# A list schedule with new prices: the same transformer trunk, its instructions in another order and partly on other engines

## The chip, the core and the metric

The kernel runs on one core of a Trainium2 chip. The metric is the device time of one execution in microseconds (us). A core has the matrix engine TensorE (PE in the profile; its weight loads are PEld), VectorE (DVE), ScalarE (ACT), GpSimd (POOL) and SyncE (SP), which here issues the DMA transfers. Each engine takes its own instructions strictly in the order in which they were issued, and waits at each for what it needs from the others.

## The reference, cut to what matters

Two layers over 512 tokens of width 1024, all in float32:

```python
for l in range(DEPTH):
    h = rms_norm(x, g_pre_mix[l])
    proj = h @ w_in[l]
    u_pool, q, k, v, iq, ik, iw = jnp.split(proj, SPLIT_POINTS, axis=-1)
    ...                                             # partial rotary embedding of q, k, iq, ik
    a_out = pool_mixer(u_pool, w_pool[l], pool_scale[l])
    b_out = dsa_attention(q, k, v, iq, ik, iw, topk)    # indexer scores, top 128 keys, softmax
    mix = jnp.concatenate([a_out, b_out], axis=-1) @ w_out[l]
    x = x + rms_norm(mix, g_post_mix[l])
    h = rms_norm(x, g_pre_ffn[l])
    f = jnp.square(jax.nn.relu(h @ w_ff1[l])) @ w_ff2[l]
    x = x + rms_norm(f, g_post_ffn[l])
```

## The kernel before

Every float32 product is made of three matmuls on operands split into a high part (a rounding copy) and a low part (a subtraction). The weights stream in: a DMA brings two chunks of 128 rows into a raw tile `wraw` (two such tiles), then for each chunk one copy and one subtraction write the two parts into a tile `ws`, of which there are eight. There are 200 chunks in a layer: 8 for the indexer (584 columns), 8 each for q, k, v and the pooling columns, 32 for `w_out`, 128 for the feed-forward part.

The text below calls the part of a layer from its first norm to the end of the `w_out` product and the next norm the **mix** (PE's products of the projections run beside DVE's indexer scores `sc`, the top-k selection `m`/`bias`, the rotary embedding `rt`, the splits `ihl`, `khl`, `qd` and the softmax `s`), and the rest the **feed-forward part**. The tiles `hT` and `A` belong to the norms before a product, `pn`, `rstd` and `x` to those after one, `facc` is the feed-forward sum, `fr` and `f1` its hidden values.

No engine's order is written by hand. The program is written down once, in program order; a recorder turns each call into an operation with a price in ns, an engine (or several that could take it) and the tiles that it reads and writes. The class `Planner` then runs a list schedule: 40 sweeps forward and backward in time, with prices from `cost`, hand-over times between engines from `LATENCY`, DMA times from `DMA_STARTS` and `DMA_LANDS`, and issues the instructions in the order of the best sweep. So the only thing that a table entry changes is the order on each engine's queue, and which of the possible engines takes an instruction. Three helpers leave that choice open: `tt` (an elementwise operation of two inputs in SBUF, DVE or POOL), `copy` (ACT or DVE) and `scaled` (DVE or ACT). Where there is a choice, `sooner` compares the time at which each engine would be done. The first way listed is the preferred one where time is short; another way is taken when the instruction would still be done `SPARE` ns before it is needed.

In the profile all these instructions have the line of the recorder (L349), so they are told apart by tiles.

Of the kernel before, what the change touches and what calls it, by code (L numbers as in the profile page):

```python
# [13 lines left out]
F32R = mybir.dt.float32r  # L14
# [67 lines left out]
class Planner:  # L82
    """Takes the instructions down in program order, finds what each depends on from the tiles that it
    reads and writes, and issues them in the order of a list schedule over the engines: of the
    instructions that an engine could start, the one with the longest chain of work behind it."""

    LATENCY = {("pe", "pe"): 0, ("pe", "act"): 197, ("pe", "dve"): 197,
               ("act", "act"): 34, ("act", "dve"): 152, ("act", "pe"): 377, ("act", "pool"): 170,
               ("dve", "dve"): 127, ("dve", "act"): 128, ("dve", "pe"): 362, ("dve", "pool"): 203,
               ("pool", "pool"): 102, ("pool", "dve"): 74, ("pool", "act"): 100, ("pool", "pe"): 309}  # L90
# [4 lines left out]
    SPARE = 4000.0  # L95
# [3 lines left out]
    NOISE = 500.0  # L99

# [40 lines left out]
    def either(self, *ways):  # L141
        """One instruction that several engines can take: each way makes one call."""
        self.collected = []
        for way in ways:
            way()
        found, self.collected = self.collected, None
        self.record([(e, c, f) for e, c, f, _, _ in found], found[0][3], found[0][4])
# [43 lines left out]
    def issue(self):  # L191
        """Sweeps forward and backward over the program in turn, each sweep taking its order of
        preference from the times of the one before, and issues in the order of the best. The first
        order is that of the longest chains behind, with a little noise to part equal ones."""
# [10 lines left out]
        for i in range(n - 1, -1, -1):  # L205
            e, cost, _ = ops[i][0][0]
            tail = 0.0
            for j, hard in succ[i]:
                tail = max(tail, rank[j] + (self.lag(e, ops[j][0][0][0]) if hard else -cost))
            rank[i] = cost + tail  # L210
# [15 lines left out]

    def sweep(self, key, pred, succ, late, fixed=None):
        """A list schedule. With ``fixed``, the ways are given and time runs backward."""
# [5 lines left out]
        for ways, _, _ in ops:  # L234
            for e, _, _ in ways:
                free[e], waiting[e], able[e] = 0.0, [], []

        def release(i):
            for w, (e, cost, _) in enumerate(ops[i][0]):
# [18 lines left out]
        def sooner(t, i, w):  # L258
            """Whether another engine should take instruction i."""
            mine = t + ops[i][0][w][1]  # L260
            for v, (e, cost, _) in enumerate(ops[i][0]):
# [18 lines left out]
        short = False  # L280
        while left:
# [34 lines left out]
            start[i], end[i], way[i] = t, t + ops[i][0][w][1], w  # L316
# [19 lines left out]
class _Recorder:  # L336
# [3 lines left out]
    def __getattr__(self, method):  # L340
        def call(*args, **kw):
            out = kw["out"] if "out" in kw else args[0]
            writes = [out] + ([kw["accum_out"]] if kw.get("accum_out") is not None else [])
            if method == "tensor_tensor_reduce":
# [4 lines left out]
                   lambda: getattr(self.real, method)(*args, **kw))  # L349
# [4 lines left out]
        return call  # L354

    def cost(self, method, args, kw, out, reads):
# [8 lines left out]
        if self.name == "pe":  # L365
            if method == "transpose":
                return 56 if args[1].dtype == F32R else 109
            return max(n / 2.4 + 2.5, 107 if free(args[1]) > 64 else 56)
# [8 lines left out]
        if self.name == "pool":  # L377
            if method == "memset":
                return 50
            return (70 + 1.2 * n) if method == "tensor_scalar" else (464 if n == 1 else 50 + 2.3 * n)  # L380
# [4 lines left out]
class WeightStream:  # L385
    """Chunks of weights in the order of their use: loaded, split into two float32r parts, and held
    in a ring until their last use."""
# [21 lines left out]
    def add_paired(self, src, r0, nrows, c0, ncols):  # L409
        """Chunks of 256 rows: rows r and r + 128 side by side."""  # L410
# [59 lines left out]
def hymba_trunk(ctx: ExitStack, tc: tile.TileContext, x, positions, g_pre_mix, w_in, w_pool,  # L470
# [60 lines left out]
    def tt(out, a, b, op, first="dve"):  # L531
        """an elementwise instruction on SBUF, on VectorE or GpSimd"""
# [3 lines left out]
    def copy(out, a):  # L536
        """a copy, on ScalarE or VectorE"""
        planner.either(lambda: act.activation(out, a, AF.Copy), lambda: dve.tensor_copy(out, a))

    def scaled(out, a, by):  # L540
        """rows times a scalar of each, on VectorE or ScalarE"""
# [109 lines left out]
    def square(out, a, total):  # L651
        """total = the sum of (a / 32) ** 2 along the row: a half's part of the row's mean square"""
        act.activation(out, a, AF.Square, scale=1.0 / 32.0, accum_out=total)

    def rstd_of(parts):
        """parts: [P, 2], the two halves' parts of the row's mean square"""
# [5 lines left out]
    def pre_norm(t, gain):  # L662
        """A[:, :, :, tile t] = the two parts of (RMSNorm(x[t]) * gain) transposed."""
# [22 lines left out]
    def post_norm(t, halves, gain, in_sbuf=False):  # L686
        """x[t] += RMSNorm(halves) * gain"""
# [21 lines left out]
    def rope(row, t, heads):  # L709
        """in place on the first 16 of each head's 64 columns."""  # L710
# [8 lines left out]
    def heads_stacked(dst_hl, row, heads):  # L719
        """dst[128, heads, 2, 64]: the two parts of each head side by side."""  # L720
# [4 lines left out]
    def heads_doubled(dst, row, heads):  # L725
        """dst[128, 2, heads, 2, 64]: either part of each head, twice side by side."""
# [4 lines left out]
    def transposed(dst, srcs):  # L731
        """dst [128, n, 128] <- transposes of n blocks of [128, 128] in float32r."""
# [14 lines left out]
    for l in range(DEPTH):  # L747
# [11 lines left out]
        # indexer projection, logits and scores  # L759
# [103 lines left out]
        # attention  # L863
# [118 lines left out]
        # feed-forward  # L982
# [102 lines left out]
```

## Time and profile before

| | before |
|---|---|
| runs | 1223.18, 1225.15, 1226.14 us; median 1225.15 |
| profiled execution | span 1222.7 us, 2.45 us under the median of the runs; no other time of that execution is given |
| PE, PEld busy | 1178.5 us (96%), 978.3 us (80%) |
| DVE busy | 777.1 us (64%) |
| ACT busy | 358.5 us (29%) |
| POOL busy | 668.5 us (55%) |
| instructions | 16265 |
| DMA | 115.41 MB, mean 94 GB/s |

A span runs from the first to the last instruction. An engine counts as busy while one of its instructions runs. A matmul's record is longer than the distance to the next one (in the feed-forward part 1393 of them start in 323 us, 0.232 us apart, while one record takes some 0.39 us), so a busy PE hides gaps shorter than about 0.16 us.

### The profile page before, as it was taken

To read this page: it belongs to the slowest core of one execution; us is meant where nothing else is said; L and a number is where in the kernel's file an instruction comes from. 1 tells how busy PE (TensorE), PEld (TensorE's weight loads), DVE (VectorE), ACT (ScalarE), POOL (GpSimd) and SP (SyncE) were. 2 spreads that over 40 slices of the span, in tenths; PEclk is the share of its full clock that TensorE was granted. 3 is DMA by queue.
4 is the path that set the end of the run, shared out by engine and by line. 5 is a ranking of instruction groups with operands and counts; after the bars stand their busy time and mean duration, and the time that the engine had idled before them with its cause. 6 is when DMAs were issued, how large, how long until landed. Compare 5 with 4: busy or idle time off the path is not lost.

```text
span 1222.7 us, 16265 instructions
## 1 busy us (share of the span) xinstructions
PE 1178.5 (96%) x5880; PEld 978.3 (80%) x5880; DVE 777.1 (64%) x1620; ACT 358.5 (29%) x840; POOL 668.5 (55%) x628
## 2 busy tenths in 40 slices
PE   5999999999999999999989999999999999999996
PEld 5987878788888888888887878787888888888885
DVE  8899999875216335245779999998632353343344
ACT  5444677540010000000354367675201000000011
POOL 4145331358659659558334543314785695684782
PEclk9999999999999999999999999999999999999999
DMA  7222222433332322332322222234234223323221
GB/s 242 70 56 67 69 69 88 138 105 121 106 101 69 121 86 71 119 93 90 113 70 69 69 69 69 71 104 138 86 104 121 87 83 107 104 86 104 87 87 69
DMA packets 62160, 115.41 MB, mean 94 GB/s; under 512 B 5248, under 2 KB 10368, under 8 KB 62080
## 3 DMA queue, kind: packets, MB, share of 16 engines
q1 hardware_dynamic: 62080, 114.38, 29.9%
q8 instruction: 46, 0.75, 0.3%
q14 instruction: 34, 0.28, 0.1%
HBM read 112.27 MB, written 2.10 MB: 94 GB/s over the span
## 4 chain that ended last, share of the span: by engine, by line
PE 68%; DVE 23%; issue 5%; POOL 1%; DMA 1%; ACT 0%; DVEq 0%; SPq 0%; POOLq 0%; ACTq 0%
PE pg L349 58%; DVE ws L349 4%; DVE bias L349 3%; PE pi L349 2%; DVE m L349 2%; PE pf L349 2%; DVE mx L349 2%; DVE sc L349 2%; DVE x L349 1%; DVE s L349 1%; DVE A L349 1%; DVE h L349 1%; DVE pT L349 1%; PE lg L349 1%; PE pool L349 1%
## 5 line engine op out<-in xcount | busy, mean ns | idle before, releaser
L349 POOL TENSOR_TENSOR ws<-wraw,ws 128x512 fp32r<-128x512 f32 x296 | 397.6, 1350 | 278.0 <-DVE ws L349 233.3
L349 DVE CAST ws<-wraw 128x512 fp32r<-128x512 f32 (+1 forms) x317 | 195.3, 624 | 337.1 <-PE pg L349 247.4
L349 PE MATMUL pg<-A,ws 128*128 128x512 f32 x1344 | 313.9, 395 | 0.0
L349 PEld LDWEIGHTS pg<-A,ws 128*128 128x128 f32 x1344 | 252.3, 188 | 60.0
L349 PE MATMUL pg<-ws,A 128*128 128x512 f32 x864 | 226.3, 400 | 1.9 <-DVE pn L349 1.6
L349 PE MATMUL pg<-ws,f 128*128 128x512 f32 x768 | 187.0, 394 | 0.0
L349 PEld LDWEIGHTS pg<-ws,A 128*128 128x128 f32 x864 | 156.9, 188 | 33.5 <-DVE pn L349 2.5
L349 PEld LDWEIGHTS pg<-ws,f 128*128 128x128 f32 x768 | 144.1, 188 | 33.6
L349 ACT ACTIVATE fr<-pg 128x512 f32<-128x512 f32 x49 | 27.9, 598 | 475.9 <-PE pg L349 475.1
L349 PE MATMUL pg<-ws,f1h 128*128 128x512 f32 x512 | 149.5, 394 | 0.0
L349 PEld LDWEIGHTS pg<-ws,f1h 128*128 128x128 f32 x512 | 96.1, 188 | 22.5
L349 POOL TENSOR_TENSOR rstd<-rstd,neg_half 128x1 f32<-128x1 f32 x32 | 25.9, 809 | 119.5 <-DVE rstd L349 114.9
L349 PE MATMUL pg<-ws,f1l 128*128 128x512 f32 x256 | 89.1, 393 | 0.0
L349 DVE TENSOR_TENSOR ws<-wraw,ws 128x512 fp32r<-128x512 f32 (+1 forms) x104 | 79.0, 772 | 0.9 <-ACT ws L349 0.5
L349 POOL TENSOR_TENSOR fr<-fr 128x512 f32<-128x512 f32 (+1 forms) x70 | 71.3, 1033 | 12.8 <-ACT fr L349 11.8
L349 ACT ACTIVATE s<-s,st 128x384 f32<-128x384 f32 (+3 forms) x96 | 54.0, 568 | 36.0 <-DVE st L349 32.5
L349 PE MATMUL pi<-ws,A 128*128 128x292 f32 x384 | 60.7, 305 | 2.2 <-DVE ws L349 1.8
L349 ACT ACTIVATE ws<-wraw 128x512 fp32r<-128x512 f32 (+1 forms) x83 | 51.9, 632 | 30.1 <-PE pg L349 19.8
L349 PE MATMUL pool<-A,ws 128*128 128x512 f32 x192 | 58.7, 407 | 0.0
L349 PEld LDWEIGHTS pg<-ws,f1l 128*128 128x128 f32 x256 | 48.1, 188 | 11.2
L349 PEld LDWEIGHTS pi<-ws,A 128*128 128x128 f32 x384 | 53.4, 190 | 3.7 <-DVE ws L349 2.4
L349 DVE CAST f1h<-fr 128x512 fp32r<-128x512 f32 (+1 forms) x40 | 39.2, 997 | 19.0 <-POOL fr L349 19.0
(154 smaller groups left out, 1493.7 us busy)
## 6 DMA issues: line engine op xcount, KB each, us to landing
wraw<-in_w_ff_dram SPq DMA_DIRECT2D x128, 512.0 KB, 3.7
wraw<-in_w_out_dram SPq DMA_DIRECT2D x32, 512.0 KB, 3.6
wraw<-in_w_in_dram SPq DMA_DIRECT2D x24, 512.0 KB, 3.6
wraw<-in_w_in_dram SPq DMA_DIRECT2D x8, 584.0 KB, 4.1
wraw<-in_w_in_dram SPq DMA_DIRECT2D x16, 256.0 KB, 3.0
x<-in_x_dram SPq DMA_DIRECT2D x4, 512.0 KB, 6.3
out_dram<-x SPq DMA_DIRECT2D x8, 256.0 KB, 2.0
gain<-in_g_pre_mix_dram SPq DMA_DIRECT2D x2, 512.0 KB, 4.7
```

The source lines that it names most:

```text
L349: lambda: getattr(self.real, method)(*args, **kw))
```

## The change

The program, its tiles and its arithmetic stay as they are. Changed are the planner's numbers and rules.

- Prices: a 512-column matmul costs 4.5 + 512/2.25 = 232 ns in the schedule in place of 215.8, small ones 60 or 111 in place of 56 or 107; a POOL elementwise operation 50 + 2.35 per column in place of 50 + 2.3, the one-column power 520 in place of 464.
- Hand-over times: to PE 240 ns from any engine in place of 309 to 377; PE to ACT and DVE 215 in place of 197; smaller moves between the others.
- `SPARE` is 20 us in place of 4 us.
- `copy` lists DVE first and ACT second; before it was the other way round.
- The forward sweeps know a port that DVE and POOL share. A method `port` gives each instruction a kind (0: does not use it; 1: uses it; 2: a DVE copy or row scaling with both sides in SBUF), and `shared` delays or lengthens it: kind 2 on DVE starts only when POOL is done and keeps POOL out until it ends; kind 1 on DVE becomes longer by 35% (`SLOWED`) of the time that it shares with POOL; a POOL instruction beside a DVE one becomes 10% longer.

```diff
-    LATENCY = {("pe", "pe"): 0, ("pe", "act"): 197, ("pe", "dve"): 197,
-               ("act", "act"): 34, ("act", "dve"): 152, ("act", "pe"): 377, ("act", "pool"): 170,
-               ("dve", "dve"): 127, ("dve", "act"): 128, ("dve", "pe"): 362, ("dve", "pool"): 203,
-               ("pool", "pool"): 102, ("pool", "dve"): 74, ("pool", "act"): 100, ("pool", "pe"): 309}
+    LATENCY = {("pe", "pe"): 0, ("pe", "act"): 215, ("pe", "dve"): 215,
+               ("act", "act"): 34, ("act", "dve"): 152, ("act", "pe"): 240, ("act", "pool"): 190,
+               ("dve", "dve"): 127, ("dve", "act"): 128, ("dve", "pe"): 240, ("dve", "pool"): 165,
+               ("pool", "pool"): 102, ("pool", "dve"): 100, ("pool", "act"): 150, ("pool", "pe"): 240}
...
-    SPARE = 4000.0
+    SPARE = 20000.0
...
+    SLOWED = 0.35
...
+    def shared(self, e, port, t, cost, held):
+        if e == "dve":
+            if port == 2:
+                t = max(t, held["pool"])
+                held["both"] = t + cost
+            else:
+                cost += self.SLOWED * min(cost, max(0.0, held["pool"] - t))
+            held["dve"] = t + cost
+        else:
+            t = max(t, held["both"])
+            if held["dve"] > t:
+                cost *= 1.1
+            held["pool"] = t + cost
+        return t, cost
...
-            start[i], end[i], way[i] = t, t + ops[i][0][w][1], w
+            cost, port = ops[i][0][w][1], ops[i][0][w][3]
+            if fixed is None and port:
+                t, cost = self.shared(e, port, t, cost, held_port)
+            start[i], end[i], way[i] = t, t + cost, w
...
+    def port(self, method, out, reads):
+        if self.name == "pool":
+            return 0 if method == "memset" else 1
+        if self.name != "dve" or any(a.space == bass.MemoryType.PSUM for a in [out] + reads):
+            return 0
+        if method in ("tensor_copy", "tensor_scalar"):
+            return 2
+        return 1 if method in ("tensor_tensor", "scalar_tensor_tensor") else 0
...
-            return max(n / 2.4 + 2.5, 107 if free(args[1]) > 64 else 56)
+            return max(4.5 + n / 2.25, 111 if free(args[1]) > 64 else 60)
...
-        planner.either(lambda: act.activation(out, a, AF.Copy), lambda: dve.tensor_copy(out, a))
+        planner.either(lambda: dve.tensor_copy(out, a), lambda: act.activation(out, a, AF.Copy))
```

Which engine splits the weight chunks, counted from the two orders (copy, then subtraction; "mix" is all chunks before the feed-forward ones):

| stage | copies before | copies now | subtractions before | subtractions now |
|---|---|---|---|---|
| layer 0 mix, 72 | DVE 35, ACT 37 | DVE 23, ACT 49 | DVE 43, POOL 29 | DVE 56, POOL 16 |
| layer 0 feed-forward, 128 | DVE 122, ACT 6 | DVE 25, ACT 103 | DVE 13, POOL 115 | DVE 39, POOL 89 |
| layer 1 mix, 72 | DVE 36, ACT 36 | DVE 26, ACT 46 | DVE 39, POOL 33 | DVE 54, POOL 18 |
| layer 1 feed-forward, 128 | DVE 124, ACT 4 | DVE 99, ACT 29 | DVE 9, POOL 119 | DVE 110, POOL 18 |

The first place is the program's start on SP's queue, where `x0` and `gain` feed the first norm, `wraw` is the first weights and `posi` the positions for the rotary tables. Before:

```order
L349 DMA x0_111<-in_x_dram 128x1024
L349 DMA posi_142<-in_positions_dram 128x4x1
L349 DMA gain_116<-in_g_pre_mix_dram 128x1024
L349 DMA wraw_117<-in_w_in_dram 128x2x584
L349 DMA x1_112<-in_x_dram 128x1024
L349 DMA wraw_118<-in_w_in_dram 128x2x584
```

Now:

```order
L371 DMA x0_111<-in_x_dram 128x1024
L371 DMA gain_116<-in_g_pre_mix_dram 128x1024
L371 DMA wraw_117<-in_w_in_dram 128x2x584
L371 DMA x1_112<-in_x_dram 128x1024
L371 DMA wraw_118<-in_w_in_dram 128x2x584
L371 DMA posi_142<-in_positions_dram 128x4x1
```

The positions went behind the second pair of weights, and the gain moved up one place. DVE at the same place, where `ropebuf` is the rotary tables' arithmetic, before:

```order
L349 TENSOR_TENSOR ropebuf_145<-posf_143,invt_144 128x32
L349 TENSOR_SCALAR ropebuf_145<-ropebuf_145 128x32 x2
L349 TENSOR_TENSOR ropebuf_145<-ropebuf_145 128x32
L349 SCALAR_TENSOR_TENSOR rstd_148<-ss_147 128x1
L349 TENSOR_SCALAR ropebuf_145<-ropebuf_145 128x32 x3
L349 TENSOR_TENSOR h_146<-x0_111,gain_116 128x512 x2
L349 TENSOR_TENSOR ropebuf_145<-ropebuf_145 128x32
L349 TENSOR_SCALAR h_146<-h_146,rstd_148 128x512
L349 CAST ws_119<-wraw_117 128x584
```

Now:

```order
L371 SCALAR_TENSOR_TENSOR rstd_148<-ss_147 128x1
L371 TENSOR_TENSOR h_146<-x0_111,gain_116 128x512 x2
L371 TENSOR_SCALAR h_146<-h_146,rstd_148 128x512
L371 CAST ws_119<-wraw_117 128x584
L371 TENSOR_TENSOR ws_119<-wraw_117,ws_119 128x584
L371 TENSOR_TENSOR ws_120<-wraw_117,ws_120 128x584
L371 TENSOR_TENSOR A_115<-hT_149,A_115 128x4x128
L371 TENSOR_TENSOR h_151<-x1_112,gain_116 128x512
```

The rotary arithmetic no longer stands among the first norm's instructions; the cast of the positions, which opens it, stands 14 rows further down.

The second place is DVE in layer 1's mix, from the scores of the second token tile (`sc1`) to the split `ihl_1095` of the third tile's indexer row, for which PE waits. Before:

```order
L349 CAST ws_1124<-wraw_996 128x512
L349 COPY irow_1092<-pi_1090 128x292
L349 SCALAR_TENSOR_TENSOR sc1_1073<-relu_1081,iw_1065,sc1_1073 128x256
L349 SCALAR_TENSOR_TENSOR sc1_1073<-relu_1083,iw_1065,sc1_1073 128x256
L349 TENSOR_TENSOR rt_1094<-irow_1092,cosT_140 128x144
L349 SCALAR_TENSOR_TENSOR sc1_1073<-relu_1085,iw_1065,sc1_1073 128x256
L349 CAST ws_1126<-wraw_1122 128x512
L349 TENSOR_TENSOR irow_1092<-rt_1094 128x9x8
L349 SCALAR_TENSOR_TENSOR sc1_1073<-relu_1087,iw_1065,sc1_1073 128x256
...
L349 CAST ws_1127<-wraw_1122 128x512
L349 TENSOR_TENSOR ihl_1095<-irow_1092,ihl_1095 128x8x64
```

Now:

```order
L371 COPY irow_1092<-pi_1091 128x284
L371 TENSOR_TENSOR ws_1127<-wraw_1122,ws_1127 128x512
L371 TENSOR_TENSOR rt_1094<-irow_1092,cosT_140 128x144
L371 SCALAR_TENSOR_TENSOR sc1_1073<-relu_1083,iw_1065,sc1_1073 128x256
L371 TENSOR_TENSOR rt_1094<-irow_1092,sinT_141 128x144
L371 SCALAR_TENSOR_TENSOR sc1_1073<-relu_1085,iw_1065,sc1_1073 128x256
L371 TENSOR_TENSOR ws_1130<-wraw_1125,ws_1130 128x512
L371 CAST ihl_1095<-irow_1092 128x8x64
L371 SCALAR_TENSOR_TENSOR sc1_1073<-relu_1087,iw_1065,sc1_1073 128x256
L371 TENSOR_TENSOR ihl_1095<-irow_1092,ihl_1095 128x8x64
```

The weight copies left DVE here (ACT has them), and weight subtractions that POOL made came to DVE; in layer 1's indexer stage POOL's queue now holds one weight subtraction (`ws_1129`) where it held five.

The third place is the end of DVE's queue: the last bank `pg_1844` is added to `facc`, multiplied by the gain (`pn_1854`), and the last token tile's `x3` is written. Before:

```order
L349 TENSOR_TENSOR facc_1601<-pg_1843,facc_1601 128x512
L349 TENSOR_TENSOR pn_1854<-facc_1601,gain_1549 128x512
L349 TENSOR_TENSOR pn_1851<-facc_1601,gain_1549 128x512
L349 SCALAR_TENSOR_TENSOR rstd_1853<-ss2_1852 128x1
L349 TENSOR_TENSOR facc_1601<-pg_1844,facc_1601 128x512
L349 SCALAR_TENSOR_TENSOR x2_113<-pn_1851,rstd_1853,x2_113 128x512 x2
L349 SCALAR_TENSOR_TENSOR rstd_1856<-ss2_1855 128x1
L349 SCALAR_TENSOR_TENSOR x3_114<-pn_1854,rstd_1856,x3_114 128x512 x2
```

Now:

```order
L371 TENSOR_TENSOR facc_1601<-pg_1843,facc_1601 128x512
L371 SCALAR_TENSOR_TENSOR x1_112<-pn_1848,rstd_1850,x1_112 128x512
L371 TENSOR_TENSOR pn_1851<-facc_1601,gain_1549 128x512
L371 SCALAR_TENSOR_TENSOR rstd_1853<-ss2_1852 128x1
L371 TENSOR_TENSOR facc_1601<-pg_1844,facc_1601 128x512
L371 TENSOR_TENSOR pn_1854<-facc_1601,gain_1549 128x512
L371 SCALAR_TENSOR_TENSOR x2_113<-pn_1851,rstd_1853,x2_113 128x512
L371 SCALAR_TENSOR_TENSOR rstd_1856<-ss2_1855 128x1
L371 SCALAR_TENSOR_TENSOR x2_113<-pn_1851,rstd_1853,x2_113 128x512
L371 SCALAR_TENSOR_TENSOR x3_114<-pn_1854,rstd_1856,x3_114 128x512 x2
```

One half of `pn_1854` stands right behind the last addition on DVE (POOL has the other half, ahead of it), and the last `rstd` stands between the two halves of `x2`.

## Rows read from the trace of the kernel before

**Rows 1.** Windows by stage: length, busy us (instructions) of PE, PEld, DVE, ACT, POOL, clock, DMA.

```profile
0.00:25.00 25.00, 12.21 (x71) 10.36 (x72) 19.82 (x47) 13.44 (x29) 11.00 (x40) 1.00 0.79 251
25.00:277.00 252.00, 244.14 (x1433) 208.38 (x1433) 231.71 (x582) 142.98 (x347) 90.88 (x109) 1.00 0.27 85
50.00:215.00 165.00, 159.98 (x863) 131.60 (x861) 162.52 (x437) 97.82 (x232) 60.10 (x75) 1.00 0.23 72
277.00:600.00 323.00, 323.00 (x1393) 261.21 (x1392) 135.74 (x187) 22.43 (x43) 221.31 (x174) 1.00 0.32 99
600.00:880.00 280.00, 265.63 (x1552) 228.68 (x1551) 255.97 (x615) 156.40 (x374) 112.49 (x122) 0.99 0.27 82
...
880.00:1200.00 320.00, 320.00 (x1382) 259.04 (x1381) 120.82 (x173) 19.04 (x35) 226.71 (x179) 1.00 0.31 96
```

**Rows 2.** Waits of the whole span: who waited for whom, us, times, longest.

```profile
DVE ws L349 <- DMA wraw<-in_w_ff_dram: 72.1, 24, 6.1
...
PE hT L349 <- DVE h L349: 13.0, 4, 9.4
...
PE hT L349 <- DVE rstd L349: 2.6, 1, 2.6
PE pi L349 <- DVE ws L349: 1.8, 3, 0.7
```

**Rows 3.** Timeline of the start: start, length, instruction, idle before it and releaser.

```profile
1.65 0.50 SPq L349 DMA_DIRECT2D gain<-in_g_pre_mix_dram  x1
...
7.46 1.29 DVE L349 TENSOR_TENSOR h<-x,gain 128x512 f32<-128x512 f32 x2 [1.22 <-DMA gain<-in_g_pre_mix_dram]
...
18.47 0.63 PE L349 MATMUL hT<-identf,h 128*128 128x128 f32 x4 [1.08 <-DVE ropebuf L349]
```

**Rows 4.** Timeline of layer 1's indexer stage.

```profile
648.20 0.47 DVE L349 SCALAR_TENSOR_TENSOR sc<-relu,iw,sc 128x256 f32<-128x256 f32 x1
...
649.09 1.30 POOL L349 TENSOR_TENSOR ws<-wraw,ws 128x512 fp32r<-128x512 f32 x1 [1.88 <-DVE ws L349]
649.30 2.29 DVE L349 SCALAR_TENSOR_TENSOR sc<-relu,iw,sc 128x256 f32<-128x256 f32 x2
...
653.14 1.48 DVE L349 SCALAR_TENSOR_TENSOR sc<-relu,iw,sc 128x256 f32<-128x256 f32 x1
...
656.04 0.54 PE L349 MATMUL tr<-ident,ihl 128*128 128x128 f32 x4 [3.03 <-DVE ihl L349]
```

**Rows 5.** DVE by form, 0 to 277 us: count, busy us, mean ns.

```profile
L349 DVE TENSOR_TENSOR ws<-wraw,ws 128x512 fp32r<-128x512 f32 x44 | 32.2, 747 | 0.2
L349 DVE CAST ws<-wraw 128x512 fp32r<-128x512 f32 x37 | 18.1, 494 | 2.7 <-DMA wraw<-in_w_out_dram 2.4
...
L349 DVE CAST qd<-qrow 128x512 fp32r<-128x512 f32 x7 | 2.9, 408 | 0.0
```

**Rows 6.** DVE by form, 600 to 880 us.

```profile
L349 DVE TENSOR_TENSOR ws<-wraw,ws 128x512 fp32r<-128x512 f32 x41 | 30.4, 751 | 0.2
L349 DVE CAST ws<-wraw 128x512 fp32r<-128x512 f32 x40 | 23.5, 592 | 5.4 <-PE pi L349 2.3 <-PE pg L349 1.9 <-DMA wraw<-in_w_out_dram 1.1
L349 DVE SCALAR_TENSOR_TENSOR x<-pn,rstd,x 128x512 f32<-128x512 f32 x14 | 13.0, 960 | 0.4 <-POOL rstd L349 0.4
...
L349 DVE SCALAR_TENSOR_TENSOR sc<-relu,iw,sc 128x256 f32<-128x256 f32 x7 | 5.6, 796 | 0.2
```

**Rows 7.** Instructions that write `ws`, 600 to 880 us: ns min/median/max, DVE, then POOL.

```profile
L349 DVE TENSOR_TENSOR ws<-wraw,ws x48: 667/683/1764, 602.5 to 876.0; 128x512 fp32r<-128x512 f32 x41, 128x584 fp32r<-128x584 f32 x7
...
L349 POOL TENSOR_TENSOR ws<-wraw,ws x35: 1276/1299/2056, 614.1 to 879.0; 128x512 fp32r<-128x512 f32 x34, 128x584 fp32r<-128x584 f32 x1
```

**Rows 8.** Timeline of the end.

```profile
1207.78 5.74 PE L349 MATMUL pg<-ws,f 128*128 128x512 f32 x24
...
1215.30 2.42 DVE L349 SCALAR_TENSOR_TENSOR x<-pn,rstd,x 128x512 f32<-128x512 f32 x2
1215.40 1.76 POOL L349 TENSOR_TENSOR pn<-facc,gain 128x512 f32<-128x512 f32 x1
...
1218.44 1.41 DVE L349 SCALAR_TENSOR_TENSOR x<-pn,rstd,x 128x512 f32<-128x512 f32 x2 [0.66 <-POOL rstd L349]
```

More of the change, by code (lines that the diff above doesn't have):

```diff
@@ L146, in either @@
         found, self.collected = self.collected, None
-        self.record([(e, c, f) for e, c, f, _, _ in found], found[0][3], found[0][4])
+        self.record([way[:4] for way in found], found[0][4], found[0][5])
     def record(self, ways, writes, reads):
@@ L205, in issue @@
         for i in range(n - 1, -1, -1):
-            e, cost, _ = ops[i][0][0]
+            e, cost = ops[i][0][0][:2]
             tail = 0.0
@@ L234, in sweep @@
         for ways, _, _ in ops:
-            for e, _, _ in ways:
+            for e, *_ in ways:
                 free[e], waiting[e], able[e] = 0.0, [], []
         def release(i):
-            for w, (e, cost, _) in enumerate(ops[i][0]):
+            for w, (e, cost, *_) in enumerate(ops[i][0]):
                 if fixed and fixed[i] != w:
@@ L260, in sooner @@
             mine = t + ops[i][0][w][1]
-            for v, (e, cost, _) in enumerate(ops[i][0]):
+            for v, (e, cost, *_) in enumerate(ops[i][0]):
                 if v == w:
@@ L280, in sweep @@
         short = False
+        held_port = {"pool": 0.0, "dve": 0.0, "both": 0.0}
         while left:
@@ L348, in call @@
             way = (self.name, self.cost(method, args, kw, out, reads),
-                   lambda: getattr(self.real, method)(*args, **kw))
+                   lambda: getattr(self.real, method)(*args, **kw), self.port(method, out, reads))
             if self.planner.collected is not None:
@@ L366, in cost @@
             if method == "transpose":
-                return 56 if args[1].dtype == F32R else 109
-            return max(n / 2.4 + 2.5, 107 if free(args[1]) > 64 else 56)
+                return 59 if args[1].dtype == F32R else 109
+            return max(4.5 + n / 2.25, 111 if free(args[1]) > 64 else 60)
         if self.name == "act":
@@ L379, in cost @@
                 return 50
-            return (70 + 1.2 * n) if method == "tensor_scalar" else (464 if n == 1 else 50 + 2.3 * n)
+            return (70 + 1.2 * n) if method == "tensor_scalar" else (520 if n == 1 else 50 + 2.35 * n)
         nbytes = math.prod(c for _, c in out.ap) * 4
```

## The prediction

> **What bounds the kernel now.** I read the windows by stage first, since the shares of the whole span mix stages with different limits. In the two feed-forward parts PE is busy for the whole stretch, 323.00 of 323 us and 320.00 of 320 [rows 1]: the other engines split weights beside it and none of their time is seen. That is over half of the span, and an order can't shorten it. In the mixes the reader is to see two full engines: between 50 and 215 us DVE is busy for 162.5 of 165 us while PE is busy for 160.0 [rows 1]. PE's idle time is 252.0 - 244.1 = 7.9 us from 25 to 277 us and 280.0 - 265.6 = 14.4 us from 600 to 880 us, together 22.3 us [rows 1]; ahead of them stand 12.8 us in the first 25 us [rows 1], of which 9.4 are the wait for the first norm [rows 2]; and after the last matmul, which ends at 1207.78 + 5.74 = 1213.5 us, 9.2 us remain to the end of the span [rows 8]. So what an order can win is 22 us in the mixes and a little at both ends.
>
> Then the list of waits: where PE waits it is for DVE [rows 2]. And the timeline shows why DVE is late: an instruction of 0.47 us takes 2.29 us for two, and 1.48 us for one, where a GpSimd subtraction of 1.30 us lies beside it [rows 4]. The same loss is in the means: weight copies on DVE take 494 and 592 ns against 408 for the same form that meets little [rows 5, 6], while DVE's median subtraction is 683 ns and its longest 1764 [rows 7].
>
> **The change part by part.** The sum is made against the profiled execution (span 1222.7 us) and its differences are then taken from the median of the runs, 1225.15.
>
> *The feed-forward parts: 0.* In layer 0 ACT takes 97 copies from DVE (6 to 103), in layer 1 DVE takes 101 subtractions from POOL (9 to 110). What hides them is PE's own work: layer 1's DVE, busy for 120.8 of 320 us [rows 1], gets 101 x 0.683 = 69 us more and is still at about 60%. If that cover fails, PE waits at a bank; this is a rival below.
>
> *The start: -2.5 us.* The gain's DMA was issued at 1.65 us, behind the 0.47 us of the positions' issue, and the first product of the norm waited for its landing at 7.46 us [rows 3]; it moves up by one issue. I take -0.5 for the first matmul, which comes at 9.4. Behind it PE waited 1.8 us in three pieces for split weights on DVE and 1.1 us behind the rotary arithmetic [rows 2, 3], which now stands lower in DVE's queue. Together 0.5 + 1.8 + 1.1 = 3.4 us at most; nothing at least, if the rotary tables are then late for the first indexer row. I take 2.5, since the tables' first user, the first token tile's `irow`, needs all eight weight chunks of the indexer first.
>
> *DVE's work in the mixes: -2.4 us.* From the table of the weight splits: POOL loses 13 + 15 = 28 subtractions, DVE gets them, at the present mean of 0.75 us [rows 5, 6] 28 x 0.75 = +21.0. DVE loses 12 + 10 = 22 copies, 22 x 0.408 = -9.0. Outside the weight and feed-forward tiles the order leaves DVE 11 instructions fewer (the most are five copies of `qd`), at the same 0.408 -4.5. That makes +7.5. Against it stands what DVE loses to POOL. Five groups show it, count times mean less the undisturbed time: 44 x (747 - 683) and 37 x (494 - 408) ns in layer 0; 41 x (751 - 683), 40 x (592 - 408), 7 x (796 - 470) and 14 x (960 - 705) ns in layer 1, the 705 being half of an undisturbed pair [rows 4 to 8]. That is 2.8 + 3.2 + 2.8 + 7.4 + 2.3 + 3.6 = 22.1 us. POOL's busy time in the mixes (11.0 + 90.9 + 112.5 = 214.4 us [rows 1]) falls by 28 x 1.30 = 36 us, 17%; its weight subtractions there fall from 62 to 34, by 45%. Lower bound of the relief: 17% of 22.1 = 3.8. Upper bound: all of it, if what remains on POOL is put where DVE does nothing that it disturbs. I take 45%, 9.9, because the long subtraction is what stands beside the stretched instructions. Net 7.5 - 9.9 = -2.4, between +3.7 and -14.6.
>
> *Two waits that hang on a stretched DVE instruction: -5.6 us.* At the second place of the order, PE waited 3.03 us for `ihl` [rows 4]. DVE lost 2.29 - 0.94 = 1.35 and 1.48 - 0.47 = 1.01 us ahead of it; now POOL has one weight subtraction in this stage in place of five, and DVE's own exchange there is small (a few subtractions against as many copies). The other is the 2.6 us before `hT` at the layer's start, behind an `rstd` [rows 2]. Both can stay (0) or other waits of the 22.3 us can go too; I take these two, 3.0 + 2.6.
>
> *The end: -1.0 us.* The last two additions to `x2` took 2.42 us beside a POOL product, and an undisturbed pair 1.41 [rows 8]. Now DVE makes the last half of that product itself, right behind the last addition, so 1.0 us goes; between 0 and 2 (the last `rstd` also comes forward).
>
> *The other prices* have no term of their own: they act only through the order.
>
> Sum: -2.5 - 2.4 - 5.6 - 1.0 = -11.5 us. From 1225.15 this is 1213.6 us, 0.9% less.
>
> A rule speaks against this. The Trainium skill, page "SBUF — State Buffer", section "SBUF: two separate sides", says that VectorE and GpSimd share a pair of ports as an exclusive lock: a DVE instruction with two inputs in SBUF, too, waits until a GpSimd instruction is done, and does not share. By that rule the planner's 35% is too little for a subtraction, and the sum would be that of the first rival. Of the rows, the longest subtraction agrees with the page: 1764 ns is an undisturbed one of 683 and most of a GpSimd one of 1299 [rows 7]. The mean of 751 [rows 6] says that few meet.
>
> **The rivals.**
> *Slower: the subtractions that came to DVE run into POOL.* Priced as lengthened by 35% of the overlap, they may be put beside the 34 weight subtractions and the other work that POOL keeps. If each of the 28 waits for half of a 1.30 us instruction, 0.65 in place of the 0.07 in the mean, DVE gets +16.3 us; with the -2.4 this is +14, and the two waits stay. 1225.15 - 2.5 - 1.0 + 14 = 1236. The lock of the Trainium skill's page "SBUF — State Buffer" would make it so wherever the two meet. It decides from 7 us of net growth on DVE. For it: DVE is full there, and the longest instruction shows that full waits occur [rows 1, 7]. Against it: POOL has less to meet, and in 85 of them the mean loss was under 0.07 us [rows 5, 6].
> *No measurable difference: what the mixes gain is lost in the feed-forward parts.* ACT, which emptied PE's banks at once, has the copies in the same queue, and copies wait for weights: DVE's did so 24 times, up to 6.1 us [rows 2]. If each of the 16 blocks of hidden values lost 0.6 us to a copy ahead of it, 10 us come back: 1225.15 - 11.5 + 10 = 1223.7. Against it: a bank and a weight tile are both freed by PE's progress, so the plan keeps their order even when it is late.
> *A larger gain.* If the schedule with truer prices leaves no PE idle time in the mixes, -22.3, with -3.4 and -2 at the ends: 1197.5. For it speaks that every price of PE was too low by some 7% (215.8 planned, 232 in the rows: 323 us for 1393 matmuls [rows 1]). Against it: PE and DVE are both nearly full, and an order must fit both.
>
> **How the numbers follow.** Likeliest 0.55, with its own range from 1205 (two thirds of the larger gain) to 1221; the larger gain 0.14, 1197 to 1205; no measurable difference 0.18; slower 0.13. About 0.3%, 3.7 us, is what a measurement of this kernel can tell from no change. Faster is 0.55 + 0.14 = 0.69. From 1200 to 1228 leaves out the slower case and half of the larger gain, 0.2.
>
> **What would show it.** The first `hT` at about 8.9 us instead of 9.4 and no wait behind `ropebuf` in the first 25 us; POOL's busy time in the mixes down to some 175 us; weight copies on DVE there nearer to 408 than to 592 ns; no wait of some 3 us before `tr`; both feed-forward parts still with PE full; about 8 us from the last matmul to the end. It would be wrong if DVE's mean subtraction in the mixes goes well above 0.75 us, if PE shows idle time between 277 and 600 us, or if PE's idle time in the mixes stays near 22 us although DVE got faster: then it was not DVE that held it.

## The result: 0.7% slower, where 0.9% faster was predicted

The changed kernel takes 1232.92 us (1232.19 to 1234.36) against 1224.22 us of the kernel before beside it: a ratio of 1.007, 95% interval 1.0056 to 1.0084. Its profiled execution, the slowest of the four runs (1234.36), has a span of 1232.6 us. The windows by stage, cut at 285 and 890 us in place of 277 and 880, since the work is later (columns as in [rows 1]):

```profile
0.00:25.00 25.00, 15.43 (x91) 14.10 (x92) 19.33 (x33) 14.47 (x31) 12.31 (x41) 1.00 0.80 262
25.00:285.00 260.00, 245.63 (x1414) 209.40 (x1413) 233.88 (x589) 156.52 (x372) 70.89 (x92) 0.99 0.26 81
285.00:600.00 315.00, 315.00 (x1357) 254.34 (x1356) 85.82 (x115) 88.43 (x148) 152.73 (x118) 1.00 0.31 98
600.00:890.00 290.00, 276.96 (x1588) 236.21 (x1587) 256.36 (x614) 171.76 (x410) 90.72 (x109) 0.99 0.27 84
890.00:1200.00 310.00, 310.00 (x1337) 250.82 (x1336) 167.07 (x253) 44.71 (x81) 56.82 (x43) 1.00 0.31 98
```

Both feed-forward parts are full as before. The start is better: PE idles for 9.6 us of the first 25, not 12.8. Layer 0's mix is worse, 260.0 - 245.6 = 14.4 us idle for 7.9, and layer 1's a little better, 13.0 for 14.4 [rows 1]. The list of waits says where (PE's waits, with total, times and longest as in [rows 2]):

```profile
PE hT L371 <- ACT h L371: 8.8, 3, 8.0
PE tr L371 <- ACT kS L371: 3.7, 1, 3.7
PE tr L371 <- DVE ihl L371: 2.6, 4, 1.3
...
PE tr L371 <- ACT khl L371: 2.5, 1, 2.5
...
PE tr L371 <- DVE khl L371: 1.7, 1, 1.7
```

The longest wait before `tr` behind `ihl`, 3.03 us [rows 4], is down to 1.3, and the first `hT` comes at 8.0 in place of 9.4. New are three waits in the evacuation of the k projection (1.65 and 3.70 us in layer 0, 2.5 us in layer 1). `evac_k` copies a bank to `krow`, applies the rotary embedding (`rt`), splits it (`khl`), transposes it on PE (`tr`) and copies the result to `kS`. The timeline of that place in layer 0:

```profile
109.65 2.74 POOL L371 TENSOR_TENSOR ws<-wraw,ws 128x512 fp32r<-128x512 f32 x2
...
111.17 1.76 DVE L371 TENSOR_TENSOR khl<-krow,khl 128x512 fp32r<-128x512 f32 x1
112.35 0.90 POOL L371 TENSOR_TENSOR rt<-krow,sinT 128x128 f32<-128x128 f32 x1
112.86 0.55 DVE L371 MAX8 m<-bias 128x8 f32<-128x384 f32 x1
...
113.08 0.50 PE L371 MATMUL tr<-ident,khl 128*128 128x128 f32 x4 [1.65 <-DVE khl L371]
113.21 2.56 POOL L371 TENSOR_TENSOR ws<-wraw,ws 128x512 fp32r<-128x512 f32 x2
113.33 1.31 DVE L371 TENSOR_TENSOR rt<-krow,cosT 128x128 f32<-128x128 f32 x1
...
114.02 1.17 PE L371 MATMUL pg<-ws,A 128*128 128x512 f32 x4
114.56 1.76 DVE L371 TENSOR_TENSOR khl<-krow,khl 128x512 fp32r<-128x512 f32 x1
...
117.21 0.63 ACT L371 ACTIVATE khl<-krow 128x512 fp32r<-128x512 f32 x1 [4.88 <-DVE krow L371]
...
118.26 1.06 ACT L371 ACTIVATE kS<-tr 128x512 fp32r<-128x512 f32 x2
...
118.89 0.75 PE L371 MATMUL tr<-ident,khl 128*128 128x128 f32 x4 [3.70 <-ACT kS L371]
...
120.46 1.92 PE L371 MATMUL pg<-ws,A 128*128 128x512 f32 x4
```

A split of 0.67 us takes 1.76 twice, since it runs only when POOL's weight subtraction is over; `rt` waits on POOL's queue behind two of them; and on ACT the copy `kS` stands behind a `khl` that waited 4.88 us for `krow`. PE has four matmuls of its own left, then waits. Behind the wait the same four matmuls take 1.92 us in place of 1.17: the granted clock fell to 0.50, which is 1.2 GHz. Three such stretches of the changed kernel, the second with the wait ahead of it (ahead of the first PE had waited for 0.67 us, ahead of the third for 2.45):

```profile
40.20:43.61 3.41, 3.36 (x14) 3.36 (x15) 2.14 (x9) 0.93 (x2) 0.49 (x2) 0.50 0.02 5
114.02:118.89 4.87, 1.17 (x6) 0.64 (x5) 4.87 (x12) 1.68 (x4) 1.75 (x2) 0.98 0.65 203
118.71:122.12 3.41, 3.23 (x13) 2.73 (x14) 3.41 (x10) 1.81 (x4) 0.00 (x0) 0.50 0.01 5
716.04:722.87 6.83, 6.41 (x26) 5.28 (x26) 6.32 (x12) 2.87 (x6) 3.69 (x4) 0.50 0.42 120
```

Of the kernel before there is one such stretch ahead of the end, behind a wait of 1.9 us:

```profile
787.48:790.89 3.41, 3.14 (x15) 3.17 (x16) 2.48 (x13) 1.02 (x3) 0.00 (x0) 0.50 0.43 148
```

So 13.65 us at 1.2 GHz in place of 3.41: at most (13.65 - 3.41) / 2 = 5.1 of the 9.9 us between the two spans. Idle time is another 2.0 (+5.1 in the mixes net, -3.2 at the start, +0.1 at the end); 2.8 us remain that no row places. These stretches differ from execution to execution: over the four runs the mean granted clock lies between 0.992 and 0.996.

### The profile page after: what moved, and what is told of

Same layout as the page of the kernel before. It is cut to its first block, busy times and chain, and to the rows that moved or that the text cites. A ratio compares the mean times of both kernels' runs of the same rounds, so it can differ in the third digit from the quotient of the medians.

```text
span 1232.6 us, 16141 instructions
## 1 busy us (share of the span) xinstructions
PE 1186.3 (96%) x5880; PEld 983.5 (80%) x5880; DVE 778.9 (63%) x1627; ACT 480.8 (39%) x1054; POOL 388.0 (31%) x407
## 4 chain that ended last, share of the span: by engine, by line
PE 73%; DVE 18%; issue 3%; ACT 2%; DMA 2%; POOL 1%; POOLq 0%; DVEq 0%; SPq 0%; ACTq 0%
PE pg L371 61%; DVE ws L371 4%; DVE bias L371 3%; PE pi L371 2%; DVE m L371 2%; PE pf L371 2%; PE pool L371 2%; DVE sc L371 2%; PE po L371 2%; PE tr L371 1%; PE s L371 1%; DVE x L371 1%; PE pt L371 1%; DVE s L371 1%; PE hT L371 1%
## 5 line engine op out<-in xcount | busy, mean ns | idle before, releaser
L371 POOL TENSOR_TENSOR ws<-wraw,ws 128x512 fp32r<-128x512 f32 (+1 forms) x141 | 193.6, 1375 | 380.4 <-DVE ws L371 195.4
L371 ACT ACTIVATE ws<-wraw 128x512 fp32r<-128x512 f32 (+1 forms) x227 | 141.4, 632 | 324.8 <-PE pg L371 253.5
L371 PE MATMUL pg<-ws,A 128*128 128x512 f32 x864 | 231.8, 404 | 2.2 <-DVE pn L371 1.3
L371 DVE TENSOR_TENSOR ws<-wraw,ws 128x512 fp32r<-128x512 f32 (+1 forms) x259 | 202.0, 791 | 16.9 <-ACT ws L371 12.9
L371 DVE CAST ws<-wraw 128x512 fp32r<-128x512 f32 (+1 forms) x173 | 82.5, 478 | 189.7 <-PE pg L371 160.7
L371 PE MATMUL pg<-ws,f 128*128 128x512 f32 x768 | 191.1, 394 | 0.0
L371 DVE TENSOR_TENSOR facc<-pg,facc 128x512 f32<-128x512 f32 x48 | 31.4, 687 | 79.7 <-PE pg L371 79.6
L371 ACT ACTIVATE s<-s,st 128x384 f32<-128x384 f32 (+3 forms) x102 | 57.9, 570 | 34.4 <-DVE st L371 33.5
L371 POOL TENSOR_TENSOR fr<-fr 128x512 f32<-128x512 f32 (+1 forms) x41 | 40.6, 1007 | 94.4 <-ACT fr L371 63.7
L371 POOL TENSOR_TENSOR rstd<-rstd,neg_half 128x1 f32<-128x1 f32 x32 | 21.6, 677 | 114.1 <-DVE rstd L371 113.9
```

The costliest lines, as they stand in the source:

```text
L371: lambda: getattr(self.real, method)(*args, **kw), self.port(method, out, reads))
```

## The experiments

All times are medians; each ratio is against the kernel before, run beside it, with a 95% interval. The theories are named in the expectations. **1**: VectorE's two-input instructions wait out GpSimd's. **2**: luck of one order. **3**: the new hand-over times. **4**, formed after the first four runs: the old, too low TensorE price was a slack.

**Four subtractions moved by hand.** `issue` gives four named operations to VectorE after the plan is made:

```diff
+        for i in (849, 863, 879, 893):
...
+            way[i] = [w[0] for w in ops[i][0]].index("dve")
         for i in sorted(range(n), key=lambda i: (start[i], i)):
```

> The changed kernel with four GpSimd weight subtractions of the k projection's evacuation in layer 0 (the ones at 109.7 and 113.2 us of its trace, two each) given to VectorE at the same places of the order; nothing else moves. Theory 1 (VectorE's two-input instructions wait out GpSimd's in full, and this is the place where it costs most): the two 1.76 us subtractions of khl go to 0.68, the waits of 1.65 and 3.70 us before tr shrink to under 2 together, the drop of the granted clock behind them goes, and the time falls by 4 to 8 us, to 1225 to 1229. Theory 2 (order luck: this scheduler's orders scatter by a per cent whatever the prices): the four subtractions add 2.7 us to a full VectorE, the stall moves on, and the time stays within 2 us of 1233. Theory 3 (hand-over to TensorE priced at 240 ns where it takes more): the waits before tr stay, since nothing of the hand-over is changed, within 2 us of 1233.

1230.01 us, ratio 1.0044 (1.0029 to 1.0059), outside all three ranges. The two `khl` splits took 0.68 us and the clock stayed at 1.00 there, as theory 1 says, but the waits fell from 1.65 and 3.70 to 1.5 and 2.2 us only. Theory 1 has the right instructions and a third of the loss, 2.9 us; the interval still overlaps that of the changed kernel (from 1.0056), so even this third is hardly clear of the noise. The clock isn't all the edit's doing: the stretch at 40.20 us, where the order is the same, is at 1.00 here too.

**The port rule as a full lock.**

```diff
-        return 1 if method in ("tensor_tensor", "scalar_tensor_tensor") else 0
+        return 2 if method in ("tensor_tensor", "scalar_tensor_tensor") else 0
```

> The changed kernel with one number of its port rule changed: two-input VectorE instructions on SBUF count as kind 2, so in the plan they wait until GpSimd is done and keep it out, in place of being lengthened by 35% of the overlap. Theory 1: the plan now fits the chip, no instruction of 0.68 us takes 1.76 on VectorE in the mixes, and the time falls below that of the kernel before, 1205 to 1220. Theory 2: some other order, 1217 to 1240 with no relation to the rule. Theory 3: the waits before tr stay as many and as long as now (about 15 us over the span), 1228 to 1236.

1241.43 us, ratio 1.0137 (1.0122 to 1.0152). All weight splits of layer 0's mix went to ACT and POOL. The windows of its first two stages:

```profile
0.00:25.00 25.00, 10.90 (x63) 9.77 (x64) 7.84 (x18) 16.84 (x34) 18.31 (x46) 1.00 0.78 254
25.00:285.00 260.00, 246.90 (x1376) 208.77 (x1375) 172.60 (x453) 168.02 (x392) 179.87 (x196) 0.97 0.27 82
```

VectorE is busy for 172.6 of 260 us, and PE still idles for 13.1, so VectorE's load doesn't set the time there. Its meetings with POOL did not go on the chip, though: in the same 260 us an addition to `x` takes 1268 ns on the mean, where an undisturbed pair took 1.41 us [rows 8]:

```profile
L371 DVE SCALAR_TENSOR_TENSOR x<-pn,rstd,x 128x512 f32<-128x512 f32 x8 | 9.8, 1268 | 0.3 <-POOL rstd L371 0.3
```

And PE idles for 14.1 us of the first 25, 4.5 more than in the changed kernel: over half of what the full lock costs is lost at the start, where POOL's queue now holds the first norm's product and two weight subtractions ahead of the power for its `rstd`. Theory 1's range is missed, but a run that keeps the meetings doesn't settle it.

**No port rule** (the condition `if fixed is None and port` made false).

> The changed kernel without the port rule (new prices, hand-over times, SPARE and the order of the copies stay). Theory 1: without any price for the port VectorE meets GpSimd more often, mean weight subtraction on VectorE in the mixes above that of the changed kernel, 1234 to 1245. Theory 2: within 8 us of 1233 on either side. Theory 3: as now, 1230 to 1236, since the hand-over prices are the cause and they stay.

1241.87 us, ratio 1.0139 (1.0122 to 1.0156): with the new prices the rule is worth 9 us. The time lies in theory 1's range, but its reason does not hold: VectorE's mean weight subtraction is 721 and 741 ns in the two mixes, below the changed kernel's 770 and 796 (shown further down). Theories 2 and 3 miss.

**Another seed** (`SEED = 54`).

> The changed kernel with another seed for the noise that parts equal chains in the first sweep (54 in place of 53). Theory 1 and theory 3: the same prices make the same kind of order, so slower than the kernel before again, 1228 to 1237. Theory 2: the time differs from 1233 by over 4 us and can fall on the other side of 1224.

1231.73 us, ratio 1.006 (1.0045 to 1.0075): 1.2 us from seed 53, with quite another order (VectorE has 1513 instructions in place of 1627). Theory 2 is weak.

**TensorE's old prices in the changed kernel.**

```diff
-                return 59 if args[1].dtype == F32R else 109
-            return max(4.5 + n / 2.25, 111 if free(args[1]) > 64 else 60)
+                return 56 if args[1].dtype == F32R else 109
+            return max(n / 2.4 + 2.5, 107 if free(args[1]) > 64 else 56)
```

> The changed kernel with TensorE's old prices (a 512-column matmul at 215.8 ns in place of 232), all else as changed. Theory 4, new (the old numbers were wrong by a slack: TensorE was planned too fast, so in the true run every other engine was ahead of it, and a late instruction seldom stopped it): the slack comes back, TensorE's idle time between 25 and 120 us falls from 8.2 us to under 4, and the time falls by 6 us or more, to 1218 to 1227. Theory 1 (waits behind GpSimd, wherever they fall): the number of meetings hardly changes, within 3 us of 1233. Theory 2 (order luck): within 3 us too, going by the 1.2 us that another seed made.

1215.92 us, ratio 0.9931 (0.9914 to 0.9949): 17.0 us from TensorE's prices, and faster than both kernels. PE's idle time between 25 and 120 us fell from 8.2 to 2.5 us. Theories 1 and 2 miss; theory 4 has the direction, with 2 us more than its range. Its windows of the mixes, and the same place of the timeline as above:

```profile
25.00:285.00 260.00, 251.60 (x1451) 213.68 (x1450) 232.78 (x573) 157.83 (x379) 89.34 (x111) 1.00 0.28 87
...
600.00:890.00 290.00, 282.64 (x1626) 241.26 (x1625) 259.93 (x602) 173.80 (x411) 116.00 (x127) 1.00 0.28 90
```

```profile
105.20 3.94 PE L371 MATMUL pg<-ws,A 128*128 128x512 f32 x16
105.22 1.78 DVE L371 TENSOR_TENSOR khl<-krow,khl 128x512 fp32r<-128x512 f32 x1
...
108.98 0.54 PE L371 MATMUL tr<-ident,khl 128*128 128x128 f32 x5
...
112.20 3.47 PE L371 MATMUL pg<-ws,A 128*128 128x512 f32 x14
...
112.93 1.47 DVE L371 TENSOR_TENSOR khl<-krow,khl 128x512 fp32r<-128x512 f32 x1
...
115.51 0.46 PE L371 MATMUL tr<-ident,khl 128*128 128x128 f32 x4
```

The same split is stretched nearly as much, 1.78 and 1.47 us. But it ends at 107.00 and 114.40, and PE comes to its transposes at 108.98 and 115.51, after 16 and 14 matmuls of its own: no wait, and no clock below 1.00 until PE's last matmul.

**The old hand-over times** (the table of before).

> The changed kernel with the old table of hand-over times (362 and 377 ns to TensorE in place of 240), all else as changed. Theory 3 (240 ns to TensorE takes away a slack that the old 362 to 377 gave): the waits before tr go, 1220 to 1227. Theory 4: the 122 to 137 ns are small against the 7% on each of TensorE's matmuls, so a part at most, 1227 to 1233. Theory 2: within 3 us of 1233.

1236.89 us, ratio 1.0104 (1.0086 to 1.0122): theory 3 falls. The new table is worth 4.0 us, which none of the expectations held.

**SPARE at 4 us.**

> The changed kernel with SPARE at 4 us in place of 20, all else as changed. The plan then leaves nearly all weight splits of the mixes to ScalarE (69 and 60 of 72 copies) and GpSimd (64 and 56 of 72 subtractions). If VectorE's own load were what stops TensorE (the prediction's view), the time falls below 1224, since about 86 subtractions of 0.68 us leave VectorE. Theory 1: GpSimd's 120 subtractions of 1.3 us then meet more VectorE instructions, 1236 to 1245. Theory 4: no slack comes back, 1230 to 1243.

1241.78 us, ratio 1.0137 (1.012 to 1.0154). Again less work on VectorE (211.9 + 242.7 us in the mixes for 233.9 + 256.4) and a longer time, so the prediction's view falls; theories 1 and 4 both hold it in their ranges.

**The port rule alone in the kernel before.**

> The kernel before with the port rule alone (35%, as in the change); prices, hand-over times, SPARE and the order of the copies are the old ones. The run without the rule was 9 us slower than the changed kernel, so theory 4 (the rule is right and the new prices do the harm) expects a gain over the kernel before, 1212 to 1222. Theory 1 (35% is too little and harms by placing VectorE beside GpSimd): 1225 to 1235. Theory 2: within 4 us of 1224.

1256.93 us, ratio 1.0264 (1.0248 to 1.0279): all three expectations missed. Its layer 0 feed-forward part isn't full any more, and PE waits there for ACT's evacuation of a bank (a window, and a row of the waits of the whole span):

```profile
285.00:600.00 315.00, 311.10 (x1330) 247.35 (x1329) 177.39 (x284) 39.29 (x69) 29.32 (x21) 1.00 0.30 96
```

```profile
PE pg L371 <- ACT fr L371: 6.0, 11, 0.7
```

**The old TensorE prices with seed 54.**

> The changed kernel with TensorE's old prices and seed 54. Theory 4 (TensorE planned too fast is a slack for all others): the gain isn't that of one order, so again well under the changed kernel, 1213 to 1221. Theory 2 (the 1215.9 was a lucky order): back to 1224 or more.

1215.76 us, ratio 0.9923 (0.9909 to 0.9938): not one lucky order.

**TensorE cheaper still** (`n / 2.6 + 2.5`, the small ones 52, 100 and 101).

> The changed kernel with TensorE's prices lower still, 199 ns for a 512-column matmul. Theory 4: more slack, so no slower than with 215.8, 1209 to 1217, the gain shrinking since few waits of TensorE on instructions in progress are left. A rival, that 215.8 is near a best value and the plan's order goes wrong on either side of it: 1219 to 1235.

1223.54 us, ratio 0.9987 (0.9977 to 0.9996): the rival in this expectation holds. Theory 4's range is missed: of the three prices tried, the middle one is best.

**The other engines dearer.** TensorE keeps its new prices:

```diff
-            return 70 + (0.52 if fast else 1.04) * n + 60 * scalars
+            return 1.075 * (70 + (0.52 if fast else 1.04) * n + 60 * scalars)
...
```

(and so for the other prices of VectorE, ScalarE and GpSimd).

> The changed kernel with TensorE's new prices kept and those of VectorE, ScalarE and GpSimd 7.5% higher instead; hand-over and DMA times stay. Theory 4: the ratio makes the slack, so most of the 17 us come back, 1214 to 1223. The rival that the old TensorE price acts in another way (through the DMA times, or the weight splits' due times): 1226 to 1236.

1215.58 us, ratio 0.9923 (0.9909 to 0.9938): the ratio of the prices does it, not the TensorE number.

**TensorE's new prices alone in the kernel before.**

> The kernel before with TensorE's new prices alone. Theory 4: the slack goes from the kernel before too, and without the port rule the plan has nothing for VectorE's lost time, so 1236 to 1255. Rival: the new price does harm only together with SPARE at 20 us or the new hand-over times, 1220 to 1230.

1273.21 us, ratio 1.0388 (1.0372 to 1.0403): 48.4 us, the direction of theory 4 and far above its range. PE's waits, the largest:

```profile
PE hT L349 <- DVE h L349: 16.1, 4, 8.4
PE tr L349 <- DVE ihl L349: 9.1, 4, 3.8
```

The largest all end with a result of VectorE.

**Which engine's lateness.** The factor 1.075 on VectorE's prices only, and on ScalarE's and GpSimd's only:

> The changed kernel with VectorE's prices alone 7.5% higher. If it is VectorE's lateness that the slack covers (it is the fullest engine beside TensorE, and the one that GpSimd holds up): most of the 17 us, 1215 to 1222. If ScalarE's and GpSimd's chains need it as much: about half, 1222 to 1228. If neither alone does: near 1233.

1218.02 us, ratio 0.9948 (0.9931 to 0.9964).

> The changed kernel with ScalarE's and GpSimd's prices alone 7.5% higher. The counterpart: 1228 to 1234 if VectorE is what the slack covers, 1215 to 1222 if it is the chains through the other two.

1235.11 us, ratio 1.0091 (1.0076 to 1.0106), 1.1 us above its range. It is VectorE's lateness. PE's idle time in the two mixes says the same. With VectorE dearer:

```profile
25.00:285.00 260.00, 252.35 (x1461) 214.58 (x1460) 231.03 (x577) 159.78 (x382) 89.93 (x110) 1.00 0.27 87
...
600.00:890.00 290.00, 283.58 (x1636) 243.42 (x1635) 257.09 (x603) 178.72 (x426) 103.78 (x119) 1.00 0.29 90
```

With ScalarE and GpSimd dearer:

```profile
25.00:285.00 260.00, 248.16 (x1440) 210.13 (x1439) 234.93 (x583) 155.40 (x371) 83.15 (x106) 1.00 0.26 82
...
600.00:890.00 290.00, 274.44 (x1575) 232.97 (x1574) 263.97 (x626) 166.94 (x401) 83.40 (x102) 0.99 0.26 81
```

That is 14.1 and 27.4 us of idle time, against 27.4 in the changed kernel and 15.8 with TensorE's old prices. VectorE's weight subtractions in the mixes (by form, 0 to 285 and 600 to 890 us), in the changed kernel:

```profile
L371 DVE TENSOR_TENSOR ws<-wraw,ws 128x512 fp32r<-128x512 f32 x57 | 43.0, 770 | 0.4 <-ACT ws L371 0.2
...
L371 DVE TENSOR_TENSOR ws<-wraw,ws 128x512 fp32r<-128x512 f32 x58 | 45.3, 796 | 0.4 <-ACT ws L371 0.2
```

and in the version with VectorE's prices 7.5% higher:

```profile
L371 DVE TENSOR_TENSOR ws<-wraw,ws 128x512 fp32r<-128x512 f32 x57 | 45.2, 809 | 1.6 <-ACT ws L371 1.4
...
L371 DVE TENSOR_TENSOR ws<-wraw,ws 128x512 fp32r<-128x512 f32 x62 | 47.5, 786 | 4.7 <-ACT ws L371 4.4
```

They are no shorter, 809 and 786 ns on the mean for 770 and 796, in a kernel that is 15 us faster. VectorE isn't quicker; PE comes to it later. At the place of the k projection this version shows it again:

```profile
100.89 1.31 DVE L371 TENSOR_TENSOR khl<-krow,khl 128x512 fp32r<-128x512 f32 x1
...
106.37 0.29 PE L371 MATMUL tr<-ident,khl 128*128 128x128 f32 x2
```

The stretched split ends at 102.20 us, 4.2 us ahead of its transposes. In the changed kernel PE stood waiting for it.

**The rule and SPARE, with the slack there.** The old TensorE prices without the port rule:

> The changed kernel with TensorE's old prices and without the port rule. If the rule is worth what it was with the new prices (9 us): 1222 to 1227. If the slack covers by itself what the rule prices: 1214 to 1219.

1214.78 us, ratio 0.9925 (0.9907 to 0.9944): the rule gives nothing then. The kernel before with the rule and SPARE at 20 us (GpSimd's prices are the new ones too, which the expectation doesn't say):

> The kernel before with the port rule and SPARE at 20 us; TensorE's prices, hand-over times and the order of the copies are the old ones. If the port rule alone came out at 1256.9 because of the small SPARE beside it: 1213 to 1224. If the old hand-over times or the old order of the copies do not go with the rule: 1235 to 1257.

1218.6 us, ratio 0.9954 (0.9938 to 0.9971): so the rule doesn't need the new hand-over times or the new order of the copies. Between this run and the 1256.9 us lie SPARE and GpSimd's prices (2% higher, the one-column power 12%); that it was the small SPARE is likely, but not shown apart. SPARE at 20 us alone:

> The kernel before with SPARE at 20 us in place of 4, nothing else. If that number is the useful part of the change: 1213 to 1219, like the versions with the old TensorE price. If the new order of the copies and the hand-over times are needed too: 1220 to 1227.

1223.64 us, ratio 0.9999 (0.999 to 1.0007): not the useful part by itself.

**VectorE 15% dearer.**

> The changed kernel with VectorE's prices 15% higher. If more slack on VectorE covers more waits: 1210 to 1217. If it turns, since the plan then starts TensorE's work later than VectorE allows, or sends work away that VectorE had time for: 1219 to 1228.

1218.72 us, ratio 0.9956 (0.9943 to 0.997): as with 7.5%; neither expectation.

## Why the prediction was wrong

The step that failed is the sentence "The other prices have no term of their own: they act only through the order". TensorE's prices alone are +17.0 us (1232.92 - 1215.92) in the changed kernel and +48.4 us (1273.21 - 1224.83) in the kernel before. I had even counted a truer price for a gain, in the rival of the larger gain ("every price of PE was too low by some 7%"; the rows show that for the 512-column matmul alone, and the diff moves the others by 0 to 7%). The sign is the other way. An engine that takes its instructions strictly in order, and is nearly full, stops for whatever is late; planned too fast, it came late itself, and what VectorE owed it was ready. With the true price the plan has VectorE's results ready just in time, and VectorE, whose instructions can be longer on the chip than in the plan (a split 1.76 us in place of 0.67), is late. This margin, the slack of theory 4, is seen in the traces at the k projection; for the other places it is argued from the times and PE's idle time.

| price of a 512-column matmul | the others' prices | us |
|---|---|---|
| 232 | as they are | 1232.9 |
| 232 | VectorE +7.5% | 1218.0 |
| 232 | VectorE +15% | 1218.7 |
| 232 | all three +7.5% | 1215.6 |
| 215.8 | as they are | 1215.9 |
| 199 | as they are | 1223.5 |

Six versions of the changed kernel with this margin take 1214.8 to 1218.7 us. The changed kernel itself and seven versions of it without the margin take 1230.0 to 1241.9. The luck of single orders would not part them so. Only the 199 ns fall between.

With TensorE's old prices the rest of the change is worth 1215.92 - 1225.00 = -9.1 us, near the sum's -11.5, and at the places of its terms: PE idles for 8.8 us of the first 25 in place of 12.8, for 15.8 us in the mixes in place of 22.3, and 8.2 us in place of 9.2 remain behind the last matmul. The port rule isn't what brings it: without the rule the time is the same (1214.78).

The terms one by one:

- *Feed-forward, 0*: right, 315.00 of 315 and 310.00 of 310 us.
- *The start, -2.5*: about right; 12.8 us of idle time became 9.6, with no wait behind `ropebuf`. The first `hT` gave 1.4 of it, where 0.5 was taken.
- *VectorE's work in the mixes, -2.4*: right in sign, and beside the point. POOL's busy time fell to 12.3 + 70.9 + 90.7 = 173.9 us, as forecast (175). VectorE's mean weight subtraction rose from 747 and 751 ns [rows 5, 6] to 770 and 796, one of the prediction's signs of being wrong, but other stretches went (`sc` of 128x256 in layer 1 takes 478 ns on the mean, 796 before [rows 6]). Cut where the hidden values `fr` begin and end, the mixes before and now:

```profile
0.00:256.00 256.00, 236.64 (x1339) 199.45 (x1340) 237.81 (x605) 150.38 (x362) 88.63 (x133) 1.00 0.32 101
569.00:859.00 290.00, 277.06 (x1526) 234.72 (x1525) 264.16 (x621) 154.80 (x373) 112.80 (x117) 0.99 0.28 85
```

```profile
0.00:264.00 264.00, 240.69 (x1337) 203.68 (x1338) 240.56 (x602) 161.72 (x380) 70.42 (x118) 0.99 0.31 97
578.00:868.00 290.00, 277.94 (x1518) 234.06 (x1517) 255.26 (x613) 165.60 (x395) 81.58 (x96) 0.99 0.27 83
```

  VectorE is busy for 495.8 us in place of 502.0, and still PE's idle time in the mixes rose from 22.3 to 27.4. The prediction named this sign: it was not VectorE's load that held PE. The runs with a slack have weight subtractions of the same mean (768 and 770 ns with TensorE's old prices) and are faster.
- *Two waits, -5.6*: the longest ones shrank to 1.3 and 0.9 (all that PE waits behind `ihl` from 3.6 to 2.6), but 1.65, 3.70 and 2.5 us before `tr` took their place. With the old TensorE price the term came: layer 1's mix idles for 290.0 - 282.6 = 7.4 us, 7.0 less than before [rows 1].
- *The end, -1.0*: not in the changed kernel. Its rows:

```profile
1217.58 5.72 PE L371 MATMUL pg<-ws,f 128*128 128x512 f32 x24
...
1224.64 1.55 POOL L371 TENSOR_TENSOR pn<-facc,gain 128x512 f32<-128x512 f32 x1
1224.99 1.75 DVE L371 SCALAR_TENSOR_TENSOR x<-pn,rstd,x 128x512 f32<-128x512 f32 x1
```

  One addition to `x` still takes 1.75 us beside POOL's half of `pn`, and 1232.6 - 1223.3 = 9.3 us remain, as before [rows 8].

The rival "slower" came near the time, 1236, by a mechanism that is only the occasion of it. The full waits are there, 1.76 us in place of 0.67, as the Trainium skill says (page "SBUF — State Buffer", section "SBUF: two separate sides": whichever of the two starts first has the ports for its whole instruction). By that rule the full lock in the plan should have helped, and it cost 8.5 us more; but it did not keep VectorE clear of POOL on the chip, so pricing the lock in a plan is not the same as avoiding it. The mechanism of the rival "no measurable difference", PE waiting for ACT at a bank, shows in the run with the port rule alone, beside a far longer time, and not here.

What stays open: why 199 ns is worse than 215.8; and which of the order of the copies, the hand-over times and GpSimd's prices brings the 8.9 us between SPARE alone (1223.64) and the changed kernel with neither TensorE's price nor the port rule (1214.78). That TensorE's busy time is longer than the lower clock explains was not settled either: with ScalarE and GpSimd dearer it is 1187.2 us, 8.7 more than before, at a mean clock of 0.997 for 0.996, so the clock explains none of it there.

## What to carry to other kernels

Before a price in a list schedule is made true, ask which engine its error protected: a bottleneck that is planned too fast gives every engine that feeds it a margin, and a truer price takes it away. Raise the prices of the engines that feed it by a like factor, or keep a margin on purpose; here 7.5% on VectorE's prices was worth 15 us, and on those of the other three engines 17 us. Try more than one size: 199 ns, a larger margin, gave 7.6 us back. And follow a stretched instruction to the engine that waits for it: a split of 1.78 us cost nothing where PE had 16 matmuls in between.

## What was not expected of the hardware

A wait of TensorE can cost twice. Behind 3.70 us of waiting the granted clock stood at 0.50, and four matmuls took 1.92 us in place of 1.17. It doesn't follow each wait, nor only long ones: with four subtractions moved, PE waited 1.5 and 2.2 us at the same place and the clock stayed, while a stretch at 0.50 came behind a wait of 0.67 us (at 40.20 us) and, in the kernel before, behind one of 1.9 us. Not all VectorE instructions wait for POOL: a `MAX8` took its 0.55 us beside POOL's `rt` (112.86 us in the timeline above), while `rt` on VectorE took 1.31 us beside a weight subtraction and 0.28 alone (at 107.62 us).
